# Cached keys and values of a decoder step moved through memory into longer rows, and the products on the keys begun two projections later

## The chip, the cores and the metric

The kernel runs on one core of a Trainium2 chip. The core has a matrix engine (TensorE, PE in the profile; its weight loads are PEld), a vector engine (DVE), a scalar engine (ACT), a general engine (GpSimd, POOL) and a queue engine (SyncE, SP) that here only issues DMAs. 16 DMA engines move data between the memory (DRAM tensors) and the on-chip buffer. The engines run side by side and wait for each other through semaphores. The metric is the device time of one execution in microseconds; three runs of the kernel before had a median of 1405.13 us (1403.96 to 1405.38).

## What is computed

One inference step of a one-layer decoder for a prompt of 1024 tokens and 8 sequences that each add 8 tokens to a long past. Of the layer, the attention matters here. It has three groups of four heads (width 64) with window and dilation (128, 1), (512, 4) and (2048, 16). A query at position t reads t, t−d, t−2d, ... back to t−window. For the 8 added tokens of each sequence the older keys and values come from caches:

```python
idx = Lw + jnp.arange(T)[:, None] - jnp.arange(band + 1)[None, :] * dil
kg = k_full[:, idxc].astype(F32)
vg = v_full[:, idxc].astype(F32)
s = jnp.einsum('bthd,btjhd->bthj', q.astype(F32), kg) * (HEAD_DIM ** -0.5)
p, lse = masked_softmax_stats(s, valid[None, :, None, :])
return jnp.einsum('bthj,btjhd->bthd', p, vg), lse
```

In the third group the dilation 16 is larger than the 8 new tokens, so each of the 64 sample queries (8 tokens x 8 sequences) has 128 cached keys of its own, which no other query shares. In the second group (dilation 4) queries share cached rows. The cache of a group lies in memory as position x sequence x 512 floats: 256 of the key (four heads) and then 256 of the value. So the key of one position is a run of 1 KB, and the value too. The rest of the layer (a pooling branch, gates, output projection, a feed-forward part) follows the attention.

## The kernel before

The whole layer is one program. First come the normaliser of the tokens and the projection of the pooling branch (up to about 60 us). Then a loop over the head groups in the order third, second, first (`for g in (2, 1, 0)`, L1141; group numbers in the code count from 0, so `g == 2` is the third group) computes q, k and v. In each group there are nine blocks: eight of 128 prompt tokens, b = 0 to 7, and block 8 with the 64 sample tokens. A call of `qkv_part` (L605) does one projection of one block: on PE 24 matmuls, of which those with q and k together ("wide", for blocks 1 to 5) have twice the columns. Blocks 8 and 0 are done as q, k, v in turn, blocks 1 to 5 as q with k and then v, blocks 6 and 7 as q of both, k of both, v of both. So each group has 3 + 10 + 6 = 19 projections of prompt blocks.

After a projection of q or k, ACT squares its result (L643 or L647), POOL adds a small term (L650, tile ms) and raises to the power −1/2 (L651, tile mr), and ACT scales the result by it (L656, tile qk). Transposes on PE follow (L672, tiles tqg2b, tqg1b), then scores (L689, sg2b), the running maximum on DVE (L698), the exponential on ACT (L699), transposes of the weights (L708, tpg2b), their copy from PSUM on ACT (L711) and the product with the values (L722, pog2b). L116 and L117 split a weight panel into a high and a low part on ACT and DVE. In the third group DVE also makes sums of tokens in a tile ts (L524 to L532) that SP stores to memory (L533, ts_d) before the tile is used again.

The order of the instructions on PE is that of the program. On the other engines a planner orders them by a simulated time line. `behind_pe` (L186) adds a wait for a given matmul, and so paces an instruction. `step` and `soon` run pieces of the other blocks' work between projections.

The sample queries of the third group are done by `sample_own_keys` (L849), a generator that is advanced by `own_step` (L1104), once after a projection (or in its middle, where it is wide) while the second and the first group are projected. It begins with a scaling of the queries on DVE (L862), which needs a loaded row wq. Then, for 16 pieces of four keys each: load the piece (`piece`, L840, tile pck, two DMAs of 256 KB on SP at L846, in runs of 1 KB), multiply it with the queries in four POOL instructions (L856), and add up on DVE (L869). After a softmax come 16 pieces of values (tile pcv), again four products each on POOL and sums on DVE (L894, L895). That makes 34 steps. The projections that have none are listed at L1200 and L1201.

The sample queries of the second and the first group are done by `sample_shared_keys` (L902). Its inner function `ask` (L910) loads keys (L927, from an input that is already transposed) and values (L923, tiles kt and keys, [128, 2 x 256] floats, in runs of 1 KB).

POOL issues DMAs of its own only late (L2115, from 454.9 us on: the shifted copies of the caches), on another queue than SP's.

Of the kernel before, what the change touches and what calls it, by code (L numbers as in the profile page):

```python
# [7 lines left out]
F32 = mybir.dt.float32  # L8
# [7 lines left out]
P = 128  # L16
D = 1024
SEQ = 1024
NB, NT = 8, 8
# [7 lines left out]
DIL = (1, 4, 16)  # L27
HD = 64
KPC = 4
# [8 lines left out]
def decoder_step(ctx, tc, i, o):  # L38
    nc = tc.nc
    v_, s_, g_, t_ = nc.vector, nc.scalar, nc.gpsimd, nc.tensor  # L40
    dma = nc.sync.dma_start
# [112 lines left out]
    def feed():  # L154
        while coming_up and coming_up[0]["key"] in ends_of:
            p = coming_up.pop(0)
            cs = slice(p["a"], p["a"] + 512)
            ins = split(p["wt"][:, 0, cs], p["wt"][:, 1, cs], p["raw"])
            behind_pe(ins, ends_of[p["key"]])
            if p["a"] + 512 == p["width"]:  # L160
                throttle.append(ins)
            ask_ahead()
# [21 lines left out]
    last_mm, last_norm = [None], [None]  # L184

    def behind_pe(ins, mm=None):  # L186

        tc.add_manual_dep(ins.ins, (mm or last_mm[0]).ins.name,
                          mybir.DependencyInfo(mybir.DependencyClass.Sync, mybir.DependencyReason.DATA), reason="pace")
# [17 lines left out]
    dp = pool("dram", space=DRAM)  # L207
# [14 lines left out]
    pg_d = dp.tile([8, P, H], F32, name="pg_d")  # L222
    ts_d = dp.tile([4, P, 4, H], F32, name="ts_d")
    new_d = dp.tile([NT, NB, 768], F32, name="new_d")
    so_d = [dp.tile([NT, NB, 4, 66], F32, name=f"so_d{g}") for g in range(2)]

    accs = ExitStack()
# [311 lines left out]
    ap = pb.enter_context(tc.tile_pool(name="att", bufs=1, reuse_waits="tile"))  # L539
# [300 lines left out]
    def piece(kv, j, name):  # L840
        t = rr(sp1, [P, KPC, 256], F32, name=f"pc{name}", tag="pc", bufs=2)
        src = i["cache_kv3"]
        for hf in range(2):
            a = bass.AP(tensor=src.tensor, offset=src.offset + (64 * hf + j) * DIL[2] * NB * 512 + kv * 256,
                        ap=[[512, NT * NB], [DIL[2] * NB * 512, KPC], [1, 256]])
            dma(t[64 * hf:64 * hf + 64], a)  # L846
        return t

    def sample_own_keys(qs, wq):  # L849
        g = 2  # L850
# [51 lines left out]
    def sample_shared_keys(g, qk, vt):  # L902
# [7 lines left out]
        def ask(n):  # L910
            if n >= len(order) or n in there:
                return
            bg, kv, r = order[n]
            there[n] = ts = []
            for x in range(2):
                if extra and x:
                    turn["extra"] = turn.get("extra", -1) + 1
                    t = extra[turn["extra"] % 3]
                else:
                    t = rr(sp, [P, 4 * 136], F32, name=f"kt{g}_{n}_{x}", tag="kt", bufs=3)  # L920
                if kv:
                    ts.append(t[:, :512].rearrange("p (b j) -> p b j", b=2))
                    dma(ts[x], i[f"cache_kv{g + 1}"].rearrange("(m r) b c -> r m b c", r=R)  # L923
                        [r][:, 4 * bg + 2 * x:4 * bg + 2 * x + 2, 256:])
                else:
                    ts.append(t.rearrange("p (b j) -> p b j", b=4))
                    dma(ts[x][:, :, :128], i[f"kT{g + 1}"][r, :, x, 4 * bg:4 * bg + 4, :])  # L927
# [213 lines left out]
    for g in (2, 1, 0):  # L1141
# [42 lines left out]
        for blks in ((8, 0), (1,), (2,), (3,), (4,), (5,)) + (((6, 7),) if g else ((6,), (7,))):  # L1184

            if g and 6 in blks:
                next_wts = [(place[0] + j) % 3 for j in range(3)]
                for j, after in enumerate((((7, 0, 1), (7, 0, 3), (6, 1, 1), (6, 1, 3)), ((7, 1, 1), (7, 1, 3), (6, 2, 1), (6, 2, 3)),
                                           ((7, 2, 0), (7, 2, 1), (7, 2, 2)))):
                    keys_of = [(g,) + a for a in after] + [(g - 1, 8, 1)] * (j == 2)  # L1190
                    line_up(i["w_in"][2 + 3 * j + g - 1], f"qkv{g - 1}_{j}", *keys_of)
            elif not g and 3 in blks:
                wg_first = line_up(lambda a: gate_quarter(a // 512 % 2, a // 1024), "ga0",
                                   *((0, 7, j) for j in (0, 0, 1, 1)), width=2048)
            tiles = {b: qkv_tiles(f"{g}_{b}", b == 8) for b in blks}

            for js in (((0, 1), (2,)) if blks[0] in (1, 2, 3, 4, 5) else ((0,), (1,), (2,))):
                for b in (blks[::-1] if g < 2 and js == (2,) and 8 in blks else blks):

                    own = g < 2 and (g, b, js) in ((0, 8, (0,)), (0, 8, (1,))) or g < 2 and b < 8 and (g, b, js) not in (  # L1200
                        (1, 7, (1,)), (1, 6, (2,)), (1, 7, (2,)), (0, 6, (0,)), (0, 6, (2,)), (0, 7, (2,)))  # L1201

                    def middle():
                        step()
                        if own:
                            own_step(1)

                    def quarter(q):
                        ends_of[g, b, js[0], q] = last_mm[0]
                        feed()  # L1210

                    if g == 1 and extra and (1, "keys") in done:
                        extra = []
                        natt = np_.tile([P, 8, 2, P], F32R, name="natt", tag="nat")
                        soon(lambda: in_order(0, (0, 2)), lambda: in_order(0, (4, 6)))
                    wide = len(js) == 2
                    qkv_part(g, wts, b, f"{g}_{b}", tiles[b], js, middle if wide else None,
                             quarter if g and b in (6, 7) else None)
                    feed()
                    if own and not wide:  # L1220
                        own_step(1)
                    if g < 2 and b == 8 and 0 in js:
                        dma(wrow, src_w)
                    if g == 0 and b == 8 and 2 in js:

                        sel = ap0.tile([P, 1024], F32R, name="sel", tag="smp")[:, :12 * HD]
                        pick = lambda a: lambda: behind_pe(v_.tensor_tensor(
                            sel[:, 256 * a:256 * a + 256].rearrange("p (a d) -> p a d", d=HD),
                            ident[:, 4 * a:4 * a + 4].unsqueeze(2).to_broadcast([P, 4, HD]),
                            ident[:, 12 + 4 * a:16 + 4 * a].unsqueeze(2).to_broadcast([P, 4, HD]), op=ALU.add))  # L1230
                        soon(pick(0), pick(1), pick(2))
                    if 2 in js:
                        (sample_block if b == 8 else prompt_block)(g, b, *tiles[b])
                if g == 2 and 8 in blks and js != (0,):
                    start(*((pool_branch(), "p") if 2 in js else (token_sums(), "t")), now=True)
# [981 lines left out]
```

## Time and profile before

| | |
|---|---|
| median of three runs | 1405.13 us |
| the profiled execution's own time | 1403.42 us |
| its span, first to last instruction | 1401.6 us |
| granted TensorE clock | 1.000 |
| third group's projections | about 60 to 160 us |
| second group's | about 160 to 270 us |
| first group's | about 270 to 380 us |
| moved by DMA in all | 303.57 MB, mean 217 GB/s |

The profile is of one execution. "Busy" is the time in which an engine executes an instruction; where a row ends in square brackets, the engine stood idle for that many microseconds before it, until the engine or the DMA named had finished. The chain that ended last is followed back from the last instruction, at each step to what released it. A window gives busy times in a stretch, and the share of time in which the 16 DMA engines had a packet in hand.

### The profile page before, as it was taken

What the parts mean: (1) busy time and instruction counts of PE and PEld (TensorE: products, weight loads), DVE (VectorE), ACT (ScalarE), POOL (GpSimd) and SP (SyncE); (2) the same over time, 40 slices, a digit from 0 to 9 for tenths busy, and PEclk for the clock granted to TensorE, in tenths of its full rate; (3) what the DMA queues carried; (4) which work ended last, traced back from release to release, by engine and by line L of the source; (5) the groups of instructions that cost most, each with busy time, mean ns of one, the idle gap of its engine ahead of it and who ended that gap; (6) DMA issues with size and microseconds to landing.
All of it is one profiled execution on the core that took longest, in us unless ns stands there. A gap on an engine that the chain in (4) does not pass through costs nothing.

```text
span 1401.6 us, 29306 instructions
## 1 busy us (share of the span) xinstructions
PE 1392.2 (99%) x11101; PEld 1342.7 (96%) x11101; DVE 954.3 (68%) x1714; ACT 754.5 (54%) x1778; POOL 236.2 (17%) x330
## 2 busy tenths in 40 slices
PE   9999999999999999999999999999999999999998
PEld 8988977887999999999999999999999999999998
DVE  7788744776776767875568677665665686664565
ACT  8557766687765323563336455555554544444443
POOL 0722266475500000000010000000000000000100
PEclk9999999999999999999999999999999999999999
DMA  6322788745477767965368668856758987777684
GB/s 215 117 90 102 220 228 215 216 127 144 120 254 232 253 216 250 319 227 179 130 203 285 227 221 269 269 200 210 249 189 287 325 272 261 234 243 231 206 260 168
DMA packets 184540, 303.57 MB, mean 217 GB/s; under 512 B 26567, under 2 KB 90509, under 8 KB 182350
## 3 DMA queue, kind: packets, MB, share of 16 engines
q1 hardware_dynamic: 181326, 258.04, 58.4%
q0 software_dynamic: 3072, 43.65, 9.8%
q8 instruction: 87, 1.43, 0.4%
q14 instruction: 55, 0.45, 0.1%
HBM read 231.55 MB, written 113.73 MB: 246 GB/s over the span
## 4 chain that ended last, share of the span: by engine, by line
PE 93%; DMA 2%; POOL 2%; DVE 1%; ACT 1%; issue 0%; SPq 0%; DVEq 0%; POOLq 0%
PE pz L1297 24%; PE pd L2075 24%; PE pg L1297 12%; PE ph L200 7%; PE pqk L200 5%; PE pab L1297 5%; PE pv L200 4%; PE a L328 3%; PE pq L200 1%; PE pk L200 1%; POOL pcv L856 1%; PE sg0b L689 1%; PE pog0b L722 1%; PE tpg0b L708 1%; POOL mr L651 0%; DMA ts_d<-ts 0%
## 5 line engine op out<-in xcount | busy, mean ns | idle before, releaser
L2075 PE MATMUL pd<-places 128*128 128x272 f32 x2688 | 331.7, 287 | 0.0
L2075 PEld LDWEIGHTS pd<-places 128*128 128x128 f32 x2688 | 331.6, 188 | 0.0
L116 ACT ACTIVATE places<-raw_d 128x544 fp32r<-128x544 f32 (+1 forms) x176 | 110.7, 646 | 162.7 <-DMA raw_d<-z_d 51.4
L117 DVE TENSOR_TENSOR places<-raw_d,places 128x544 fp32r<-128x544 f32 (+1 forms) x176 | 122.6, 712 | 92.4 <-ACT places L116 90.6
L2115 POOL DMA_DIRECT2D out_kv_sample_dram<-in_cache_kv_dram x96 | 47.2, 492 | 790.7 <-ACT places L116 580.9
L1297 PE MATMUL pz<-act,places 128*128 128x280 f32 (+1 forms) x1080 | 139.4, 287 | 0.0
L1297 PEld LDWEIGHTS pz<-act,places 128*128 128x128 f32 x1080 | 135.9, 188 | 0.0
L200 PE MATMUL ph<-act,places 128*128 128x280 f32 (+1 forms) x768 | 96.6, 287 | 0.0
L200 PEld LDWEIGHTS ph<-act,places 128*128 128x128 f32 x768 | 96.0, 188 | 0.1
L1297 PE MATMUL pg<-act,places 128*128 128x264 f32 (+1 forms) x576 | 75.6, 288 | 0.0
L1297 PEld LDWEIGHTS pg<-act,places 128*128 128x128 f32 x576 | 72.6, 188 | 0.6 <-issue 0.3
L1297 PE MATMUL pz<-places,apart 128*128 128x264 f32 (+1 forms) x528 | 67.9, 287 | 0.0
L1297 PEld LDWEIGHTS pz<-places,apart 128*128 128x128 f32 x528 | 66.6, 188 | 0.0
L200 PE MATMUL pqk<-places,act 128*128 128x512 f32 x240 | 60.6, 402 | 0.6 <-ACT qk L656 0.6
L1297 PE MATMUL pz<-act,apart 128*128 128x264 f32 (+1 forms) x456 | 59.2, 287 | 0.0
L1297 PEld LDWEIGHTS pz<-act,apart 128*128 128x128 f32 x456 | 57.5, 188 | 0.3 <-ACT e L1862 0.2
L200 PEld LDWEIGHTS pqk<-places,act 128*128 128x128 f32 x240 | 44.7, 192 | 10.5 <-ACT qk L656 0.8
L651 POOL TENSOR_TENSOR mr<-ms,mhalf 128x4 f32<-128x4 f32 (+2 forms) x39 | 52.9, 1356 | 3.1
L856 POOL TENSOR_TENSOR pck<-pck,qs 128x256 f32<-128x256 f32 x64 | 47.4, 774 | 29.1 <-DMA pck<-in_cache_kv_dram 24.5
L328 PE MATMUL a<-act,places 128*128 128x384 f32 (+1 forms) x288 | 50.3, 332 | 0.9 <-ACT act L306 0.4
L1297 PE MATMUL pab<-ab,places 128*128 128x264 f32 (+1 forms) x384 | 50.4, 286 | 0.0
L328 PEld LDWEIGHTS a<-act,places 128*128 128x128 f32 x288 | 47.5, 188 | 2.8 <-ACT act L306 1.2
(435 smaller groups left out, 2789.3 us busy)
## 6 DMA issues: line engine op xcount, KB each, us to landing
out_kv_sample_dram<-in_cache_kv_dram POOLq DMA_DIRECT2D x72, 480.0 KB, 4.9
raw_d<-z_d SPq DMA_DIRECT2D x112, 272.0 KB
z_d<-t SPq DMA_DIRECT2D x80, 272.0 KB
raw_d<-in_w_down_dram SPq DMA_DIRECT2D x80, 256.0 KB
raw_u<-in_w_up_dram SPq DMA_DIRECT2D x64, 256.0 KB
raw_qkv<-in_w_in_dram SPq DMA_DIRECT2D x36, 256.0 KB
pck<-in_cache_kv_dram SPq DMA_DIRECT2D x32, 256.0 KB
pcv<-in_cache_kv_dram SPq DMA_DIRECT2D x32, 256.0 KB
```

Of the source, the lines that this page charges most:

```text
L116: ins = s_.activation(dst_hi, src, AF.Copy)
L117: v_.tensor_tensor(dst_lo, src, dst_hi.bitcast(F32), op=ALU.subtract)
L200: last_mm[0] = t_.matmul(out, lhs(a, k), rhs(b, k), start=(j == 0), stop=(j == len(terms) - 1))
L328: last_mm[0] = t_.matmul(pts[m][:, :n], wt[:, a, kk, m * P:(m + 1) * P], act4[b][kk][:, :, part4(c)], start=(p == 0 and kk == 0), stop=(p ...
L651: last_norm[0] = g_.tensor_tensor(r[:n, :H], ms[:n, :H], mhalf[:n, :H], op=ALU.pow)
L689: t_.matmul(sc[e][:, hp, j * P:(j + 1) * P], qT[rows, hp, :], kT[rows, 2 + hp, :], start=True, stop=True)
L708: t_.transpose(tp[:, hp * nk + j, :], sms[e][:, hp, j * P:(j + 1) * P], ident)
L722: t_.matmul(po[e * HD:(e + 1) * HD, hp, :], vr[:, h * HD:(h + 1) * HD], pTs[e][:, hp * nk + j, :], start=(j == 0), stop=(j == nk - 1))
L856: ins = g_.tensor_tensor(out, *others, op=ALU.mult)
L1297: last_mm[0] = t_.matmul(out[c], lhs(*term), rhs(*term, c), start=(first and n == 0), stop=(n == len(terms) - 1), skip_group_check=not first)
L2075: last_mm[0] = t_.matmul(outs(chain[t], Q)[c], A[:, a, t * P:(t + 1) * P], Z[:, b, c], start=(fresh and f == 0 and n == 0), stop=(f == NG ...
L2115: ins = g_.dma_start(d, a)
```

## The change

Two sets of buffers in memory are added, 16 of 512 KB for the third group's keys (`own_d`) and 16 of 256 KB for the second group's values (`val_d`). While the third group is projected, POOL issues DMAs from memory to memory that copy the caches into them, three after each of its first 16 projections of prompt blocks: two for one piece of four keys, one for one piece of values. Each waits for the last matmul that stood ahead of the projection (`before[0]`). The pieces of keys are then loaded in one DMA with rows of 4 KB, the second group's values in rows of 2 KB. The values of the third group and those of the first are loaded as before.

The list of projections without a step of the own keys changes: block 0's q and k in the second group have none now, and block 7's k in the second group and block 6's q in the first have one. The number of steps stays 34.

```diff
+    own_d = [dp.tile([P, KPC * 256], F32, name=f"own_d{n}") for n in range(16)]
+    val_d = [dp.tile([P, 512], F32, name=f"val_d{n}") for n in range(16)]
...
     def piece(kv, j, name):
         t = rr(sp1, [P, KPC, 256], F32, name=f"pc{name}", tag="pc", bufs=2)
         src = i["cache_kv3"]
+        if not kv:
+            dma(t.rearrange("p n d -> p (n d)"), own_d[j // KPC])
+            return t
         for hf in range(2):
             a = bass.AP(tensor=src.tensor, offset=src.offset + (64 * hf + j) * DIL[2] * NB * 512 + kv * 256,
                         ap=[[512, NT * NB], [DIL[2] * NB * 512, KPC], [1, 256]])
             dma(t[64 * hf:64 * hf + 64], a)
         return t
+
+    before = [None]
+
+    def shared_values(g, bg, r, x):
+        return i[f"cache_kv{g + 1}"].rearrange("(m r) b c -> r m b c", r=DIL[g])[r][:, 4 * bg + 2 * x:4 * bg + 2 * x + 2, 256:]
+
+    def own_rows():
+        src = i["cache_kv3"]
+        row = DIL[2] * NB * 512
+        for n in range(16):
+            for hf in range(2):
+                a = bass.AP(tensor=src.tensor, offset=src.offset + (64 * hf + n * KPC) * row,
+                            ap=[[512, NT * NB], [row, KPC], [1, 256]])
+                behind_pe(g_.dma_start(own_d[n][64 * hf:64 * hf + 64].rearrange("p (n d) -> p n d", n=KPC), a), before[0])
+            r, bx = n % 4, n // 4
+            behind_pe(g_.dma_start(val_d[4 * r + bx].rearrange("p (b d) -> p b d", b=2), shared_values(1, bx // 2, r, bx % 2)),
+                      before[0])
+            yield
+
+    own_moves = own_rows()
...
-                    dma(ts[x], i[f"cache_kv{g + 1}"].rearrange("(m r) b c -> r m b c", r=R)
-                        [r][:, 4 * bg + 2 * x:4 * bg + 2 * x + 2, 256:])
+                    if g:
+                        dma(t[:, :512], val_d[4 * r + 2 * bg + x])
+                    else:
+                        dma(ts[x], shared_values(g, bg, r, x))
...
-                        (1, 7, (1,)), (1, 6, (2,)), (1, 7, (2,)), (0, 6, (0,)), (0, 6, (2,)), (0, 7, (2,)))
+                        (1, 0, (0,)), (1, 0, (1,)), (1, 6, (2,)), (1, 7, (2,)), (0, 6, (2,)), (0, 7, (2,)))
...
+                    before[0] = last_mm[0]
                     qkv_part(g, wts, b, f"{g}_{b}", tiles[b], js, middle if wide else None,
                              quarter if g and b in (6, 7) else None)
                     feed()
+                    if g == 2 and b < 8:
+                        next(own_moves, None)
```

## The prediction

> **What bounds the kernel now.** I read the page first (busy time, then the chain that ended last), then the windows by stage, then the waits of the weight loads and the timeline at the places where TensorE stops.
>
> ```profile
> span 1401.6 us, 29306 instructions
> PE 1392.2 (99%) x11101; PEld 1342.7 (96%) x11101; DVE 954.3 (68%) x1714; ACT 754.5 (54%) x1778; POOL 236.2 (17%) x330
> PE 93%; DMA 2%; POOL 2%; DVE 1%; ACT 1%; issue 0%; SPq 0%; DVEq 0%; POOLq 0%
> ...
> 63.00:78.00 15.00, 15.00 (x116) 14.23 (x117) 7.82 (x27) 8.51 (x52) 8.58 (x10) 1.00 0.18 54
> 78.00:90.00 12.00, 12.00 (x67) 10.10 (x65) 11.53 (x19) 5.97 (x35) 2.44 (x2) 1.00 0.24 81
> 90.00:101.50 11.50, 11.50 (x73) 9.90 (x72) 10.35 (x27) 7.82 (x42) 2.61 (x2) 1.00 0.21 75
> 101.50:113.00 11.50, 11.50 (x74) 9.61 (x74) 11.08 (x25) 8.05 (x44) 2.81 (x2) 1.00 0.32 120
> 113.00:125.00 12.00, 12.00 (x80) 10.19 (x79) 10.08 (x23) 7.89 (x41) 2.14 (x2) 1.00 0.38 138
> 125.00:137.00 12.00, 12.00 (x85) 10.07 (x84) 10.19 (x23) 8.48 (x43) 3.31 (x2) 1.00 0.20 70
> 170.00:260.00 90.00, 89.00 (x757) 71.21 (x756) 45.97 (x135) 56.44 (x228) 57.24 (x79) 1.00 0.88 224
> 262.00:272.00 10.00, 8.07 (x78) 6.99 (x71) 8.03 (x20) 7.25 (x22) 5.14 (x7) 1.00 0.83 229
> 410.00:420.00 10.00, 10.00 (x83) 10.00 (x82) 8.93 (x15) 7.46 (x16) 0.00 (x0) 1.00 0.97 318
> ```
>
> The columns of the windows are: stretch, its length, busy time of PE, PEld, DVE, ACT and POOL, the granted clock, the share of the DMA engines, GB/s. TensorE is busy 1392.2 of 1401.6 us, at clock 1.00, and has 93% of the chain. So nothing but idle TensorE can be won. The third group's projections (63 to 160 us) keep PE full, with DVE next (11.08 of 11.50 us) and the DMA engines at 0.18 to 0.38. In the second group (170 to 260 us) the DMA engines are at 0.88, yet PE is idle for 1.00 us of 90. The other loss is at 262 to 272 us: 1.93 us. Those idle times have causes in the timeline:
>
> ```profile
> 172.04 0.43 DVE L862 SCALAR_TENSOR_TENSOR qs<-wq,qs 128x256 f32<-128x256 f32 x1 [2.20 <-DMA wq<-in_qk_norm_dram]
> 173.94 2.80 POOL L856 TENSOR_TENSOR pck<-pck,qs 128x256 f32<-128x256 f32 x4 [3.34 <-DVE ss L873]
> 174.22 0.40 ACT L699 ACTIVATE smg2b<-smg2b,sta 128x128 f32<-128x128 f32 x1 [2.66 <-DVE sta L698]
> 174.77 0.14 PEld L708 LDWEIGHTS tpg2b<-cst,smg2b 128*128 128x128 f32 x1 [0.55 <-ACT smg2b L699]
> 175.15 0.14 PEld L708 LDWEIGHTS tpg2b<-cst,smg2b 128*128 128x128 f32 x1 [0.25 <-ACT smg2b L699]
> 178.04 0.91 ACT L656 ACTIVATE qk<-pk,mr 64x64 f32<-64x64 f32 x4 [1.63 <-POOL mr L651]
> 179.00 2.60 PEld L200 LDWEIGHTS pqk<-places,act 128*128 128x128 f32 x12 [0.83 <-ACT qk L656]
> ...
> 265.38 0.63 ACT L116 ACTIVATE places<-raw_qkv 128x512 fp32r<-128x512 f32 x1 [2.23 <-PE pv L200]
> 268.54 0.41 ACT L711 COPY pTg1b<-tpg1b 128x256 f32<-128x256 f32 x1
> 269.00 0.41 PEld L722 LDWEIGHTS pog1b<-pTg1b,v 128*64 128x64 f32 x6 [2.17 <-ACT pTg1b L711]
> ```
>
> The reader is to see two stalls. At 174 to 179 us the weight loads wait 0.55 + 0.25 + 0.83 = **1.63 us**. DVE had stood 2.20 us at L862, the first work of the third group's own keys, for a DMA; L698, L699 and the transposes came late behind it, and POOL's first four key products (2.80 us) stood ahead of the normaliser that L656 waits for. At 269 us they wait **2.17 us** for one PSUM copy, which stands in ACT's order behind a weight split (L116) that had waited for PE's own projection. Together 3.80 us, 0.27% of the time: that is about the most a change here can gain.
>
> **The change part by part.**
>
> *Key products begun two projections later.* The own-key steps of the second group's first block, parts q and k, go; two come back at its block 7, k, and the first group's block 6, q. The count stays 34, so the work is moved and not removed: each step is 4 products on POOL, a reduction on DVE and a load. What leaves the 174 to 179 us stretch is L862's wait (2.20 us), L862 and the first products. DVE, then L698 and L699, come about 2.20 + 0.43 = 2.6 us earlier, more than the 1.63 us that PE waits, and POOL's 2.80 us no longer stand ahead of mr. I take the whole 1.63 us; next late there is PE itself. Bounds: 0 (the planner puts something else there) to −1.63. The last step with keys and the softmax fall one step each into the first group, where POOL has room:
>
> ```profile
> 272.00:282.00 10.00, 10.00 (x94) 9.66 (x93) 7.75 (x14) 7.39 (x22) 1.30 (x3) 1.00 0.65 172
> ```
>
> POOL is busy 1.30 of 10 us, so 2.80 us more are covered; if they weren't, the normalisers after 282 us would be late by up to 2.8 us.
>
> *The 48 moves, on POOL.* 16 calls, one behind each of the third group's first 16 projections, issue two moves of keys and one of values, 256 KB each in 1 KB pieces from memory to memory: 12.6 MB. Each waits for a matmul that precedes its projection, so it is ready when POOL is idle, and the ms and mr (L650, L651) that follow on POOL queue behind it; ACT's L656 waits for these. No row shows a POOL move of this shape. The nearest:
>
> ```profile
> L2115 POOL DMA_DIRECT2D out_kv_sample_dram<-in_cache_kv_dram x96: 488/488/717, 454.9 to 1335.0; - x96
> L846 SPq DMA_DIRECT2D pck<-in_cache_kv_dram x32: 596/608/1007, 167.0 to 256.5; - x32
> q0 software_dynamic: 3072, 43.65, 9.8%
> L650 POOL TENSOR_TENSOR ms<-ms,stats 128x8 f32<-128x8 f32 x5 | 3.5, 696 | 45.9 <-ACT qk L647 45.9
> 71.67 0.19 POOL L650 TENSOR_TENSOR ms<-ms,stats 64x4 f32<-64x4 f32 x1 [2.41 <-ACT qk L647]
> 85.14 0.45 POOL L650 TENSOR_TENSOR ms<-ms,stats 128x8 f32<-128x8 f32 x1 [9.89 <-ACT qk L647]
> 85.67 1.99 POOL L651 TENSOR_TENSOR mr<-ms,mhalf 128x8 f32<-128x8 f32 x1
> 87.70 1.75 ACT L656 ACTIVATE qk<-pqk,mr 128x64 f32<-128x64 f32 x8 [0.40 <-POOL mr L651]
> 94.15 0.60 PE L672 MATMUL tqg2b<-cst,qk 128*128 128x128 f32 x4
> ```
>
> Lower end: 488 ns, POOL's own move (few, long pieces). Upper end: if all of that is per packet, 3072/96 = 32 packets make 15 ns each, and 256 pieces with 16 packets more 4.1 us. I take **0.61 us**, the row with the same source, bytes and pieces (L846, though on SP's queue). 48 x 0.61 = 29 us. POOL's idle time per block is 45.9/5 = 9.2 us, for 6 moves 3.7 us: covered. A normaliser that falls behind three moves is late by at most 1.8 us; its transposes have 94.15 − (87.70 + 1.75) = 4.7 us to spare. Cost 0. Cover is gone at 9.2/6 = 1.5 us a move, and at the opening, where 12 moves share 2.41 + 9.89 = 12.3 us, at 1.0 us.
>
> *The 48 moves, on the DMA engines.* q0's 43.65 MB took 9.8% of 1401.6 us: 318 GB/s. 12.6 MB are 40 us, over some 80 us in which the engines stand at about 0.3; the sum is 0.8. A call's three moves are a burst of 2.5 us. They hide behind PE; the stores that DVE waits for are the danger (below).
>
> *Larger rows in the second group.* 16 loads of 512 KB in place of 32 of 256, and 16 value loads in 2 KB rows: the same bytes, SP saves 16 x 0.61 us. PE's 1.00 us there hangs on the first stall already counted. So 0.
>
> The Trainium skill, "DMA: Bandwidth & Descriptors", Specifications, puts line rate at rows of 512 B and more, which speaks against this part: 1 KB would be enough already. Here 224/0.88 = 255 GB/s per full share at 170 to 260 us stand against 318/0.97 = 328 at 410 us, so the trace rather disagrees; by either the sum keeps a 0 here.
>
> Sum: −1.63 us. For the second stall I take 0, as none of the ACT work in front of L711 is taken away; ends −2.17 and, for another like it made by the new order, +2.17. The profiled execution took 1403.42 us (span 1401.6 and 1.8 around it), 1.7 below the median 1405.13; 1403.42 − 1.63 = 1401.8, against the median **1403.5 us**.
>
> **The rivals.**
>
> *Both stalls go.* Fewer issues on SP and quicker loads shift the order at 262 us, too: −3.80, so 1401.3 (−0.27%). For it: POOL's steps and their loads move exactly there. Against: the split that holds ACT waited for PE.
>
> *POOL becomes the bound* (slower). The place is ms and mr behind the moves; it decides at 1.0 us a move for the opening, 1.5 us for the blocks. At 1.7 us the opening lacks 12 x 1.7 − 12.3 = 8.1 us, less 4.7 spare, and each of 4 further blocks 6 x 1.7 − 9.2 = 1.0: +7.4 − 1.6 = +5.8, so 1410.9. At 4.1 us the opening lacks 36.9 us and each of the 4 blocks 15.4: about +95. For it: POOL operations already stretch here, the same 128x8 sum takes from 0.30 to 1.31 us:
>
> ```profile
> 119.90 0.30 POOL L650 TENSOR_TENSOR ms<-ms,stats 128x8 f32<-128x8 f32 x1 [9.16 <-ACT qk L647]
> 131.50 1.31 POOL L650 TENSOR_TENSOR ms<-ms,stats 128x8 f32<-128x8 f32 x1 [9.38 <-ACT qk L647]
> ```
>
> Against: L2115's minimum and median are both 488 ns.
>
> The Trainium skill, "SBUF — State Buffer", the box on DVE blocking DMA, says that a move issued from POOL can't write its descriptors while DVE runs a two-port copy, some 0.62 us becoming 3.1 us; 48 x 3.1 = 149 us would be this rival at its worst. Its section Who interferes with whom exempts a tensor_tensor, which is most of what DVE does here; no run shows it either way.
>
> *The stores wait* (slower). DVE reuses the ts tile (L524) once its store landed, and has little to spare:
>
> ```profile
> DVE ts L524 <- DMA ts_d<-ts: 3.9, 4, 1.5
> 149.06 5.91 DMA ts_d<-ts
> ```
>
> Eight stores, each behind a burst of 2.5 us, are 20 us at most; DVE is idle 59 − 53.2 = 5.8 us at 78 to 137 us. With half of them caught, 10 − 5.8 = +4.2, less 1.6: 1407.7. Against: PE has slack of its own.
>
> *The change doesn't do what it says*: the planner leaves the first products where PE waits as before. 1405.1.
>
> **How the numbers follow.** A measurement of this kernel tells 0.2% (2.8 us) from no change. Forecast 0.40, no effect 0.06, both stalls gone 0.22, POOL bound 0.19, stores 0.13. So faster 0.22, same 0.46, slower 0.32. The range: below it goes past both stalls by 0.4 us, 1400.9; above to 1412.0, which takes in the stores and POOL up to 1.7 us a move, and leaves out moves beyond that. Cases of both signs share it; the likeliest one's own range is 1402.3 to 1405.7 (−2.8 to +0.5).
>
> **What would show it.** Right: POOL's move rows at 0.5 to 1.0 us; no wait of weight loads on L699 or L656 near 175 us; L862 without a wait for wq; mr rows of the third group at most 2 us later than now; DMA share 0.6 to 0.9 at 78 to 137 us. Wrong: move rows over 1.0 us with L656 waiting for mr and PE for L656 or L672; L524 waiting for ts_d over 1.5 us; a new wait of 2 us on PE from the planner's order.

## The result, and the profile after

The changed kernel is slower. Its median is 1410.61 us (1408.06 to 1414.16, 11 runs), that of the kernel before, run beside it, 1406.71 us (1403.58 to 1409.57, 11 runs). The ratio is 1.0027, 95% interval 1.0015 to 1.0039. The forecast was 1403.5 us against 1405.13, 0.9988.

The page of the changed kernel, its first lines (span, busy time of each engine):

```profile
span 1408.4 us, 29343 instructions
PE 1394.1 (99%) x11101; PEld 1343.0 (95%) x11101; DVE 959.2 (68%) x1714; ACT 755.3 (54%) x1778; POOL 267.3 (19%) x378
```

POOL is busy 31.1 us longer (267.3 against 236.2), and has 48 instructions more: the moves. The number of matmuls is the same. The stretches that the prediction showed are these in the changed kernel (length, busy time of PE, PEld, DVE, ACT, POOL, granted clock, share of the DMA engines, GB/s):

```profile
63.00:78.00 15.00, 13.42 (x104) 12.38 (x102) 6.61 (x23) 8.57 (x57) 12.57 (x17) 1.00 0.47 148
78.00:90.00 12.00, 12.00 (x75) 10.86 (x74) 9.38 (x17) 4.50 (x26) 5.91 (x11) 1.00 0.88 280
90.00:101.50 11.50, 9.56 (x55) 7.35 (x54) 9.23 (x20) 5.52 (x35) 5.24 (x6) 1.00 0.61 196
...
137.00:160.00 23.00, 22.18 (x185) 20.61 (x185) 18.22 (x46) 18.02 (x86) 15.30 (x19) 1.00 0.90 276
170.00:260.00 90.00, 89.25 (x767) 72.01 (x766) 46.71 (x142) 57.37 (x231) 50.93 (x68) 1.00 0.72 219
262.00:272.00 10.00, 10.00 (x100) 8.32 (x98) 8.30 (x14) 6.92 (x20) 8.90 (x11) 1.00 0.89 305
```

The reader is to see where PE's column falls short of the length. Before the change PE was full from 63 to 160 us; the last of these stretches in the kernel before:

```profile
137.00:160.00 23.00, 23.00 (x191) 21.24 (x191) 17.89 (x47) 19.81 (x88) 6.42 (x8) 1.00 0.59 180
```

Now PE lacks 1.58 us at 63 to 78, 1.94 at 90 to 101.5 and 0.82 at 137 to 160. The second group at 170 to 260 us, busy in its DMA engines for 0.88 before, is at 0.72 now. The stall near 269 us is gone; in its place PE waits 1.0 us for a copy of the same kind (L713) near 282 us.

Because all kernels of this study issue the same 11101 matmuls in the same order, each matmul can be compared with itself: its start after the first matmul, less the same in the kernel before. That difference at a few places, taken as growth over a stretch of the kernel before, says where time is lost (+) or won (−):

```
us of shift against before     60 to 170   170 to 190   190 to 280   280 to the end
changed kernel                    +5.24       -0.63        -1.42        +2.98
```

So the third group loses 5.24 us, the second group wins 2.05, and a further 2.98 are lost later, spread over a stretch where the change does no more than let the own-key steps come one projection later, up to the first group's block 6. The profiled execution of before (1403.42 us) is some 3 us faster than the medians of its later runs (1405.94 to 1406.9); the sum of such a row, +6.78 with the first 60 us, reads too high by about that. The last column is the least certain: one execution of each kernel, and no experiment below takes it apart.

The three places of the third group, in the timeline of the changed kernel (start, length, engine, line; in brackets the idle time before and what ended it):

```profile
63.56 1.36 POOL L866 DMA_DIRECT2D own_d<-in_cache_kv_dram  x2 [1.20 <-PE mt L401]
65.42 3.48 POOL L404 TENSOR_TENSOR stats<-xg,mhalf 128x8 f32<-128x8 f32 x2
68.67 0.53 POOL L652 TENSOR_TENSOR ms<-ms,stats 64x4 f32<-64x4 f32 x2
69.61 1.24 POOL L866 DMA_DIRECT2D own_d<-in_cache_kv_dram  x2 [0.41 <-PE pk L624]
70.78 0.76 POOL L868 DMA_DIRECT2D val_d<-in_cache_kv_dram  x1
71.35 2.22 POOL L653 TENSOR_TENSOR mr<-ms,mhalf 64x4 f32<-64x4 f32 x2
74.10 1.72 ACT L658 ACTIVATE qk<-pq,mr 64x64 f32<-64x64 f32 x8
75.07 0.39 PE L624 MATMUL pv<-places,smp_t 128*128 128x256 f32 x1 [1.58 <-ACT qk L658]
...
89.02 1.36 DVE L526 TENSOR_TENSOR ts<-act,act 128x544 f32<-128x544 f32 x2 [2.39 <-DMA ts_d<-ts]
91.30 2.21 POOL L653 TENSOR_TENSOR mr<-ms,mhalf 128x8 f32<-128x8 f32 x1
96.55 0.27 DVE L700 CUSTOM_DVE_ANT_0 smg2b<-sg2b,cst 128x128 f32<-128x128 f32 x1
96.87 0.40 ACT L701 ACTIVATE smg2b<-smg2b,sta 128x128 f32<-128x128 f32 x1 [1.99 <-DVE sta L700]
97.27 1.73 ACT L658 ACTIVATE qk<-pqk,mr 128x64 f32<-128x64 f32 x8
98.64 0.95 PE L674 MATMUL tqg2b<-cst,qk 128*128 128x128 f32 x4 [1.86 <-ACT qk L658]
...
152.07 0.91 PE L509 MATMUL pl<-ext,lin 128*128 128x384 f32 x2 [0.82 <-DVE ext L484]
```

The same place in the kernel before:

```profile
67.00 1.00 POOL L651 TENSOR_TENSOR mr<-ms,mhalf 64x4 f32<-64x4 f32 x1
68.04 0.91 ACT L656 ACTIVATE qk<-pq,mr 64x64 f32<-64x64 f32 x4 [0.39 <-POOL mr L651]
72.48 0.52 PE L622 MATMUL pv<-places,smp_t 128*128 128x256 f32 x1
```

Six moves stand ahead of the first mr. The three of the first call, from 63.56 us on, stand ahead of POOL's work on the tokens' statistics (L404). The three of the second call, from 69.61 us on, stand between two ms and the two mr that belong to them. The mr begin at 71.35 us; before, the first was at 67.00 us (0.61 us of the difference is there on PE, too, at 60 us). ACT's scaling L658 is late behind them, at 74.10 in place of 68.04 us. PE's next projection of v needs the PSUM that L658 reads. Before, it came 3.5 us after the end of that scaling (72.48 less 68.95); now it waits 1.58 us. At 91.3 us the same order delays an mr; the planner then put L658 on ACT behind one exponential L701. This waits for L700 on DVE, and DVE had stood 2.39 us for the store of ts. PE waits 1.86 us. At 152 us PE waits 0.82 us for DVE alone. (The line numbers are higher behind the added code: L650, L651, L656, L672, L711 and L722 are now L652, L653, L658, L674, L713 and L724.)

The moves themselves, and DVE's waits for the stores between 60 and 180 us (us in total, times, longest):

```profile
L866 POOL DMA_DIRECT2D own_d<-in_cache_kv_dram x32: 585/619/742, 63.6 to 147.8; - x32
L868 POOL DMA_DIRECT2D val_d<-in_cache_kv_dram x16: 723/758/795, 64.8 to 148.4; - x16
DVE ts L526 <- DMA ts_d<-ts: 10.6, 6, 2.6
```

A move costs POOL 0.62 or 0.76 us. The stores are waited for 10.6 us in place of 3.9.

### The profile page after: what moved, and what is told of

It is laid out like the page before. It is cut to its first block, busy times and chain, and to the rows that moved or that the text cites. A ratio compares the mean times of both kernels' runs of the same rounds, so it can differ in the third digit from the quotient of the medians.

```text
span 1408.4 us, 29343 instructions
## 1 busy us (share of the span) xinstructions
PE 1394.1 (99%) x11101; PEld 1343.0 (95%) x11101; DVE 959.2 (68%) x1714; ACT 755.3 (54%) x1778; POOL 267.3 (19%) x378
## 4 chain that ended last, share of the span: by engine, by line
PE 70%; DMA 2%; DVE 1%; ACT 0%; issue 0%; SPq 0%; DVEq 0%; ACTq 0%
PE pz L1327 23%; PE pd L2105 21%; PE pg L1327 12%; PE ph L200 7%; PE pab L1327 4%; DMA raw_d<-in_w_down_dram 1%; DMA raw_d<-z_d 1%; PE pog0b L724 0%; DVE places L117 0%; PE sg0b L691 0%; PE tpg0b L710 0%; ACT places L116 0%; PE pk L200 0%; PE pv L200 0%; PE pq L200 0%
## 5 line engine op out<-in xcount | busy, mean ns | idle before, releaser
L653 POOL TENSOR_TENSOR mr<-ms,mhalf 128x4 f32<-128x4 f32 (+2 forms) x39 | 53.3, 1374 | 2.5 <-POOL ms L652 0.2
```

Of the source, the lines that this page charges most:

```text
L653: last_norm[0] = g_.tensor_tensor(r[:n, :H], ms[:n, :H], mhalf[:n, :H], op=ALU.pow)
```

## The experiments

Two theories stood against each other. **Order**: the moves delay the normalisers on POOL, and the order that the planner makes around them leaves PE waiting, whatever the moves carry. **Bytes**: 12.6 MB of copies hold up the stores and loads of the third group. Beside them stood the question of what the own steps and the longer rows bring. The shifts of all runs, as above, with the recorded ratio to the runs of before that were made beside each. (It is not the ratio of the two medians, which differs from it by up to 0.001.)

```
                     60 to 170  170 to 190  190 to 280  280 to end   ratio to before, 95% interval
changed kernel         +5.24      -0.63       -1.42       +2.98      1.0027  [1.0015, 1.0039]
e1_steps_only           0.00      -1.88       +1.21       +1.40      0.9980  [0.9971, 0.9989]
e2_moves_only          +7.78      +3.60       -2.01       +1.48      1.0049  [1.0036, 1.0062]
e3_behind_norm         +7.36      -0.50       -1.77       +1.82      1.0037  [1.0025, 1.0050]
e4_dead_moves          +7.02      -0.56       +2.90       +1.13      1.0053  [1.0039, 1.0067]
e8_short_moves         +3.69      -0.44       +1.56       -0.81      1.0011  [0.9997, 1.0024]
e9_norm_short          +5.02      -1.89       +0.47       +5.51      0.9995  [0.9982, 1.0008]
e10_values_only        +0.23      -1.88       +1.93       +2.34      0.9989  [0.9975, 1.0004]
e11_keys_only          +0.08      -1.89       -1.37       +0.74      0.9976  [0.9958, 0.9993]
e12_third_short        +2.83      -0.22       -0.66       -0.60      0.9999  [0.9987, 1.0010]
e5_moves_on_sp         +2.56      -1.50       -1.56       +0.48      0.9990  [0.9975, 1.0004]
e13_keys_old_steps     +0.32      +0.26       -2.32       +0.05      0.9991  [0.9972, 1.0010]
```

One thing in these shifts is neither order nor bytes as such. In the profiled executions of six kernels the granted clock of PE fell to 0.5 for 3.41 us right behind a stall. In e1_steps_only:

```profile
264.05:267.47 3.42, 1.44 (x12) 1.07 (x10) 2.56 (x6) 3.22 (x10) 2.49 (x4) 1.00 1.10 231
267.47:270.88 3.41, 3.03 (x15) 2.70 (x16) 3.41 (x12) 3.41 (x13) 1.51 (x3) 0.50 0.40 112
```

Over such a stretch the shift grows by 1.3 to 1.6 us more. In the first column this is in e2, e3, e4 and e9, in the second in e2, in the third in e1, e4 and e10. The kernel before, the changed kernel, e5, e8, e11, e12 and e13 have no such stretch between 60 us and the last 20 us, so they can be compared as they stand.

**The two halves of the change.** e1_steps_only is the kernel before with the new list of own steps and no move. e2_moves_only is the changed kernel with the old list.

```diff
-                        (1, 7, (1,)), (1, 6, (2,)), (1, 7, (2,)), (0, 6, (0,)), (0, 6, (2,)), (0, 7, (2,)))
+                        (1, 0, (0,)), (1, 0, (1,)), (1, 6, (2,)), (1, 7, (2,)), (0, 6, (2,)), (0, 7, (2,)))
```

> The kernel before with only the list of own-key steps changed: no move, loads as before. Order theory (the moves on POOL stand ahead of the normalisers ms and mr, which come late): the third group loses nothing, so PE comes to the second group's first projections (174.8 us before) within 0.5 us of before; the stall of 1.63 us at 174 to 179 us shrinks by 0.5 to 1.6 us and the whole is 0 to 4 us faster than before. Traffic theory (the moves' bytes delay the stores that DVE waits for): the same, as there are no moves. Chance theory (any new order of the planner costs some us): the third group may lose 2 to 5 us here as well.

> The moves and the longer rows with the own-key steps where they were before. Order and traffic theory: the third group loses what it lost in the changed kernel, 5.2 us (PE 5 to 6 us late at the second group's start), and the whole is 4 to 7 us slower than before. If the loss came from the later key steps: the third group loses nothing.

The steps alone made the kernel faster, 0.9980; the moves alone slower, 1.0049. In e1 nothing changes up to 170 us, and between 170 and 190 us 1.88 us are won: the weight loads' waits for L699 and L656 are gone. Part of it comes back behind that: +1.21 us between 190 and 280, at the second stall. There PE's weight load waits 2.6 us in place of 2.2, and 1.3 us more are lost at the halved clock behind it. So the loss belongs to the moves. (Of e2's shift up to 190 us, 2.8 us are the clock's.)

**The moves behind the normaliser.** In e3_behind_norm each move also waits for the mr of its block, so that POOL takes it up behind that.

```diff
+    def after_norm(ins):
+        behind_pe(ins, before[0])
+        behind_pe(ins, last_norm[0])
...
-                behind_pe(g_.dma_start(own_d[n][64 * hf:64 * hf + 64].rearrange("p (n d) -> p n d", n=KPC), a), before[0])
+                after_norm(g_.dma_start(own_d[n][64 * hf:64 * hf + 64].rearrange("p (n d) -> p n d", n=KPC), a))
```

> The changed kernel, but each set of three moves also waits for the normaliser mr of the projection that it follows, so that POOL takes it behind mr. Order theory: the waits of PE for the scaled q and k near 75 and 98 us (2.0 and 2.3 us) go; the third group ends at most 1.5 us later than before, and the whole is 3 to 5 us faster than the changed kernel. Traffic theory: as many bytes in the same time, DVE still waits 8 to 11 us for the stores of ts, and the third group is still 3 to 5 us late.

The two stalls at 75 and 99 us are gone; the shift does not grow at all up to 101 us. But the third group ends 7.36 us late, up to 1.6 us of it by the halved clock. The waits of PE and DVE in e3_behind_norm, 60 to 180 us:

```profile
PE pl L509 <- DVE ext L484: 2.6, 1, 2.6
PE sg2b L691 <- DVE qkTg2b L677: 1.7, 2, 1.1
...
DVE ts L526 <- DMA ts_d<-ts: 13.6, 7, 3.9
```

PE now waits for DVE, and DVE for the stores. Order explains the first two stalls, and with them gone something else of the moves still costs time. That the moves run later here, up to 160 us in place of 148, next to more of the stores, was not separated from it.

**The moves without their readers.** e4_dead_moves makes all 48 moves, but keys and values are loaded from the caches in runs of 1 KB as before the change.

```diff
-        if not kv:
-            dma(t.rearrange("p n d -> p (n d)"), own_d[j // KPC])
-            return t
...
-                    if g:
-                        dma(t[:, :512], val_d[4 * r + 2 * bg + x])
-                    else:
-                        dma(ts[x], shared_values(g, bg, r, x))
+                    dma(ts[x], shared_values(g, bg, r, x))
```

> The changed kernel, all moves made, but keys and values loaded from the caches in 1 KB rows as before, so the copies are not read. If the longer rows bring anything, this is slower than the changed kernel by that: 1 us or more. My theory: the same as the changed kernel within 1 us in the profile's stages (third group 5.2 us late), since PE waits for none of these loads.

1.0053 against 1.0027: reading the copies is worth some 3.7 us to the changed kernel. In the shifts they are seen between 190 and 280 us, +2.90 in place of −1.42 (1.5 us of e4's +2.90 are the clock's). The prediction's sum had 0 for them, and so had the theory on record for e4.

**Short moves.** e8_short_moves is e4 with only the first 32 floats of each run moved; e9_norm_short does the same behind the normaliser.

```diff
-                            ap=[[512, NT * NB], [row, KPC], [1, 256]])
+                            ap=[[512, NT * NB], [row, KPC], [1, 32]])
```

> The 48 moves stay where the changed kernel has them, but each copies only the first 32 floats of a piece (128 bytes in place of 1 KB) and nothing reads the copies: the second group's value tiles and the third group's key tiles are loaded from the caches in 1 KB pieces as before the change. Theory A, POOL's and ACT's order makes the loss of the third group: the two stalls near 75 and 99 us stay at 2.0 and 2.8 us, the third group ends some 5 us late, VectorE still waits for ts_d about as long as in e4_dead_moves (10.5 us) only if the count of pieces counts. Theory B, the bytes make the loss: the wait for ts_d falls to about 4 us as before the change, the stall behind VectorE's ext near 152 us (1.0 to 1.2 us) goes, and the third group ends 2 us earlier than with whole moves. Time by A 1.005 of before, by B 1.002.

> As e8_short_moves, but each set of moves also waits for the normaliser of its block, as in e3_behind_norm. If order and bytes together make the whole loss of the third group, then there is nothing left of it: TensorE's matmuls up to 200 us are within 1 us of before the change, VectorE's wait for ts_d is near 4 us, ScalarE's wait for sta near its value before, and the time is that of e1_steps_only, 0.997 to 0.999 of before. If the count of moves or of pieces costs by itself, the end of the third group stays 5 us or more late, as in e3 (7.6 us), and the time is 1.003 to 1.005.

With an eighth of the bytes the stall at 75 us stays (a step of 1.98 us in the shift), while what is lost from 79 to 101 us shrinks from 4.66 us in e4 (3.2 without the halved clock) to 1.52. The third group loses 3.69 us in place of 7.02 (5.55 without it). DVE's wait for ts_d is 4.5 us in place of 10.5. So both theories hold a part: neither the order nor the bytes is the whole. In e9 nothing is lost up to 140 us (0.01 us of shift), as expected, but then a single stall of 2.87 us comes, which neither theory had, and 1.6 us of halved clock behind it. ACT and PE in e9_norm_short, near it:

```profile
165.32 0.35 ACT L713 COPY pTg2b<-tpg2b 128x256 f32<-128x256 f32 x1
167.97 0.63 ACT L116 ACTIVATE places<-raw_qkv 128x512 fp32r<-128x512 f32 x1 [2.29 <-DMA raw_qkv<-in_w_in_dram]
168.51 0.35 ACT L713 COPY pTg2b<-tpg2b 128x256 f32<-128x256 f32 x1
168.91 1.11 PE L724 MATMUL pog2b<-pTg2b,v 128*64 128x128 f32 x6 [2.75 <-ACT pTg2b L713]
```

The copy that PE waits for (168.51 us) stands behind a weight split that waits 2.29 us for its load: the form of the old second stall, made anew by the planner's order. e9 says the losses up to 140 us are explained; it does not reproduce e1.

**Keys alone, values alone.** e10_values_only keeps the 16 moves of values and loads the keys as before. e11_keys_only keeps the 32 moves of keys and loads the values as before. So each has one or two moves in a step in place of three.

```diff
-            r, bx = n % 4, n // 4
-            behind_pe(g_.dma_start(val_d[4 * r + bx].rearrange("p (b d) -> p b d", b=2), shared_values(1, bx // 2, r, bx % 2)),
-                      before[0])
...
-                    if g:
-                        dma(t[:, :512], val_d[4 * r + 2 * bg + x])
-                    else:
-                        dma(ts[x], shared_values(g, bg, r, x))
+                    dma(ts[x], shared_values(g, bg, r, x))
```

(e11; e10 leaves out the loop over hf and the three lines in `piece` instead.)

> The changed kernel with the 16 moves of values alone; the third group's keys are loaded from the cache as before. A third of POOL's moves and of their bytes is left (11.6 us of POOL, 4.2 MB). If the loss goes with the moves' number, the third group ends 1 to 2 us late in place of 5; if one move ahead of a normaliser is enough for the stall, the stalls at 75 and 99 us stay at a third to the whole of 2.0 and 2.3 us. The gain of the second group near 270 us (2 us) stays if it is the value rows that bring it, and goes if it is the key rows. With both in its favour 0.997 of before, with both against it 1.003.

> The changed kernel with the 32 moves of keys alone; the second group's values are loaded from the cache as before. Two thirds of the moves stay (18.9 us of POOL, 8.4 MB). By the number of moves the third group ends 3 to 4 us late. The gain near 270 us stays if the key rows bring it and goes if the value rows do. 1.001 to 1.004 of before.

Neither loses anything in the third group: +0.23 and +0.08. With two thirds of the moves and of their bytes a loss of 3 to 4 us was expected, so the loss does not go with their number. The keys' moves bring the gain near 270 us (−1.37), the values' do not (+1.93, or +0.5 without the halved clock; e1, without any move, has −0.1 so). **e11_keys_only has the lowest ratio of the study, 0.9976**; its interval ends at 0.9993, and that of the changed kernel begins at 1.0015. Whether it beats e1_steps_only (0.9980) these runs can't tell: by the medians alone e1, e10, e11 and e13 all lie between 0.9981 and 0.9984. Its timeline at the place of the first stall:

```profile
69.35 0.62 POOL L866 DMA_DIRECT2D own_d<-in_cache_kv_dram  x1 [1.06 <-PE pk L624]
69.99 1.04 POOL L653 TENSOR_TENSOR mr<-ms,mhalf 64x4 f32<-64x4 f32 x1
70.99 0.62 POOL L866 DMA_DIRECT2D own_d<-in_cache_kv_dram  x1
71.63 1.05 POOL L653 TENSOR_TENSOR mr<-ms,mhalf 128x4 f32<-128x4 f32 x1
...
71.06 0.91 ACT L658 ACTIVATE qk<-pq,mr 64x64 f32<-64x64 f32 x4
73.83 0.97 ACT L658 ACTIVATE qk<-pq,mr 128x64 f32<-128x64 f32 x4
```

With two moves the planner puts one ahead of each mr, not all ahead of both. The first L658 begins at 71.06 us in place of 74.10, and PE does not wait.

**A third move without bytes.** e12_third_short is e11 with a third move at the place of the value move, 128 bytes a run, that nobody reads. POOL and ACT have the changed kernel's order in the third group again.

```diff
+            behind_pe(g_.dma_start(val_d[n].rearrange("p (b d) -> p b d", b=2)[:, :, :32],
+                                   shared_values(1, n // 4 // 2, n % 4, n // 4 % 2)[:, :, :32]), before[0])
             yield
```

> e11_keys_only with a third move in each step, at the place of the value move, that copies 128 bytes of each piece (0.5 MB in all) and that nobody reads. In the third group POOL's and ScalarE's instructions stand in the order of the changed kernel again, while the bytes are nearly those of e11_keys_only. Theory A, the third instruction on POOL and the order that the planner makes of it cost the changed kernel its time: the stalls near 75 us (2.0 us) and 98 us (1 to 2.3 us) are back, the third group ends 3 to 4 us late, and the time is 1.000 to 1.002 of before. Theory B, it is the bytes of the value moves: no stall at 75 and 98 us, and 0.997 to 0.998 of before as in e11_keys_only.

Theory A's stalls are back. The waits of PE and DVE in e12_third_short, 60 to 180 us:

```profile
PE pv L624 <- ACT qk L658: 1.6, 1, 1.6
PE tqg2b L674 <- ACT qk L658: 0.3, 1, 0.3
...
DVE ts L526 <- DMA ts_d<-ts: 6.7, 6, 1.7
```

The stall at 75 us is exactly that of the changed kernel (1.6 us on PE). The one at 99 us is 0.3 in place of 1.9 us: with the same order it needs DVE's long wait for a store, too. By 190 us e12 stands 4.4 us behind e11 (+2.61 against −1.81): the price of the third instruction and its order. Of these, 2.75 us are lost in the third group and 1.67 between 170 and 190 us, where no move is issued any more (the last at 146.7 us). The changed kernel stands another 2.0 us behind (+4.61): the price of the values' bytes. POOL's order is the same in both; DVE's is not, and its part in the 2.0 us is not separated. e8 does not fit quite as well: with fewer bytes than e12 it ends the third group 0.9 us later; that is left open.

**The moves on SP.** e5_moves_on_sp issues the 48 moves from SP.

```diff
-                behind_pe(g_.dma_start(own_d[n]...
+                behind_pe(dma(own_d[n]...
```

> The changed kernel with all 48 moves issued from SP's queue in place of POOL, so that no normaliser has a move ahead of it; bytes, sizes and readers as changed. Theory A: the stalls at 75 and 98 us go, and what is left is the traffic's part; from e9_norm_short and e3_behind_norm that is 1 to 3 us of waits for ts_d and ext. Time 0.998 to 1.001 of before. Theory B: the third group ends 5 us late or later, as in the changed kernel. A wait of a move on SP for its matmul holds the loads queued behind it, which can cost a stall for weights in either theory.

With every byte and no move on POOL the stalls at 75 and 99 us are gone, and what the third group loses, 2.56 us, is waited for on DVE (ts_d 8.5 us; PE waits 0.9 us for L677). The ratio is 0.9990 in place of 1.0027. This is a second measure of the bytes, beside the 2.0 us above.

**The keys' rows alone.** e13_keys_old_steps is e11 with the old list of steps.

> e11_keys_only with the list of own steps as before the change: the keys' moves and their 4 KB rows alone. If the two halves of the gain add up (the steps bring the stall of 174 to 184 us, the rows that of 269 us), the stall at 174 to 184 us is back (1.3 us or more over e11), the one at 269 us is smaller by 1 to 2 us than before the change, and the time is 0.998 to 1.000 of before. If the longer rows bring nothing, the time is 1.000 to 1.001; e4_dead_moves against the changed kernel, 1.0053 to 1.0027, speaks for 2 to 4 us by the rows of keys and values together.

As expected the first stall is back (+0.26 in place of −1.89), and the second stall is nearly gone: −2.32 us. The time, 0.9991, is not told from no change. ACT at the second stall in e13_keys_old_steps:

```profile
263.74 0.63 ACT L116 ACTIVATE places<-raw_qkv 128x512 fp32r<-128x512 f32 x1 [2.29 <-DMA raw_qkv<-in_w_in_dram]
...
265.33 1.78 ACT L603 CAST natt<-act 128x256 fp32r<-128x256 f32 x3
266.99 0.41 ACT L713 COPY pTg1b<-tpg1b 128x256 f32<-128x256 f32 x1
```

Before, a second weight split stood ahead of this copy, begun at 265.38 us, and the copy began at 268.54. Here only one stands there, and the copy begins 1.55 us earlier. So this gain came through another order on ACT; the split's own wait for its load is no shorter (2.29 us against 1.54). With the same order, e1 and e11 show the loads at work. In e1_steps_only, SP's issue of the weight panel and the split that waits for it:

```profile
257.14 0.58 SPq L127 DMA_DIRECT2D raw_qkv<-in_w_in_dram  x1
264.25 0.63 ACT L116 ACTIVATE places<-raw_qkv 128x512 fp32r<-128x512 f32 x1 [2.95 <-DMA raw_qkv<-in_w_in_dram]
```

In e11_keys_only:

```profile
256.77 0.57 SPq L127 DMA_DIRECT2D raw_qkv<-in_w_in_dram  x1
262.17 0.63 ACT L116 ACTIVATE places<-raw_qkv 128x512 fp32r<-128x512 f32 x1 [2.02 <-DMA raw_qkv<-in_w_in_dram]
```

From issue to split it is 7.1 us in e1 and 5.4 in e11, and the wait of PE's weight load for the copy behind it falls from 2.6 to 1.0 us. In e10, with the keys in runs of 1 KB too, the split waited 4.0 us for its load.

## Why the prediction was wrong

**The stall at 174 to 179 us** was forecast to go whole, −1.63 us. In e1, e10 and e11 it does: −1.88 to −1.89. In the changed kernel only 0.63 us are won, and 0.22 in e12, because the wait of PE's weight load for L658 stays (0.8 and 1.0 us). No move stands ahead of that normaliser, as the last is issued at 148.4 us. In e5 and e9 1.50 and 1.89 are won, but in e3, where the moves stand behind the normalisers as in e9, only 0.50. So the step was right by itself, and how the moves took most of it back in some kernels is not shown.

**"The 48 moves, on POOL: covered. Cost 0"** is the step that failed. The price of a move was right (0.61 forecast, 0.62 and 0.76 measured), and so was the room: POOL was not full. What failed is how the delay of mr was priced. The prediction took three moves ahead of one mr, 1.8 us, and set them against the 4.7 us that one block's transposes had to spare. The trace shows a start later by 4.35 us for the first mr (71.35 against 67.00), because six moves stand ahead of it: the planner put the first call's three ahead of L404 and the second call's three ahead of two normalisers at once, and these waited for PE besides. It shows another reader with less to spare: PE's projection of v, which needs the PSUM that L658 empties, had 3.5 us. And it shows that ACT's order moves with POOL's, so that near 99 us L658 came behind work that waits for DVE. The bound "cover is gone at 1.0 us a move" was a bound on POOL's capacity; the loss began at 0.62 us with three moves, and was nothing with two. The rival "POOL becomes the bound" named the place (L656 late behind ms and mr, PE late for L656 or L672) but not the point from which it decides. Price by e12 against e11: 4.4 us, 2.75 of it in the third group.

**"They hide behind PE; the stores that DVE waits for are the danger"**: the danger was real, together with the order. The rival gave +4.2 us; the bytes cost 2.0 us (the changed kernel against e12) or 2.56 (e5). Two thirds of the bytes in the same stretch cost 0.08 us (e11). There the stores are waited for 6.6 us, and PE does not see it.

**"Larger rows in the second group: 0"** was a term set to nothing that is worth some 2 to 4 us: −2.32 in e13 alone, 3.7 us by e4 against the changed kernel. It comes from the keys' loads, not from the values'. The prediction's sum argued that PE's 1.00 us hung on the first stall and counted the second as unchanged, with ends of 2.17 us either way; only its rival "Both stalls go" had quicker loads at the second stall, with 0.22. What of the loads did it stays open: a piece of keys was two loads of 64 partitions in runs of 1 KB out of the cache, and became one of 128 partitions in rows of 4 KB out of a compact copy. No run separates these. The queue of SP's loads from 172 to 276 us, before and in e11_keys_only (packets, MB, share of the 16 engines' time):

```profile
q1 hardware_dynamic: 29149, 22.88, 85.5%
```

```profile
q1 hardware_dynamic: 23159, 23.23, 72.7%
```

For 23 MB the engines are busy 0.727 of the stretch in place of 0.855. Per busy time that is 23.23/(0.727 x 104 us) = 307 GB/s against 22.88/(0.855 x 104) = 257. That is a rise by 19% for the whole queue; e11 has the new steps, too, and against e1, which has them without the moves, it is 307 against 265. The Trainium skill, "DMA: Bandwidth & Descriptors", Specifications, puts line rate at 512 B and more. By it rows longer than 1 KB would bring nothing; the trace shows a rise, but not that the length of the rows made it, as the loads changed in more than that.

**"Next late there is PE itself"** holds for 170 to 190 us only. The own-key work that left this stretch makes the second stall longer by 0.4 us where the keys are loaded as before (e1), and the halved clock behind it costs 1.3 us more in that execution. With the new steps and the keys' new loads together (e11) the wait is 1.0 us, and the clock stays at 1.00.

**The worst case of POOL** did not appear. The Trainium skill, "SBUF — State Buffer", A bandwidth-pool intuition that's wrong, gives about 3.1 us for a POOL-issued DMA that a copy on DVE holds up. The longest issue of the 48 moves took 0.795 us in the changed kernel and 1.025 in e3_behind_norm, with DVE busy for 9.38 of 12 us at 78 to 90 us in the changed kernel.

**The chances**: 0.32 stood on the slower side, split between the two rivals that, together, took place; they were held apart as if only one could. Both follow from one thing, a third move in each step. That the measured 1410.61 us stands so near the 1410.9 of "POOL becomes the bound" is luck: that sum took 1.7 us a move, and a move took 0.62 or 0.76.

What is left open: the 2.98 us of shift behind 280 us in the one profiled execution of the changed kernel, the 0.9 us between e8 and e12, the first stall in e3 against e9, and what of the keys' new loads makes them quicker.

## What to carry to other kernels

An engine with idle time is not free to issue DMAs: ask what its next instruction releases, on which engine that stands in what order, and who waits for the PSUM that it empties; the smallest of these margins is the price, not the engine's idle share. Where a planner orders the other engines, one instruction more can change the order of several of them, so try such an addition in doses (here two moves a step cost nothing and three cost over 4 us) before it is judged. Longer and fewer loads were worth making here for the keys, whose loads crowd a busy stretch (32 of 256 KB became 16 of 512 KB), and brought nothing for the values. And before shifts between two profiles are compared, look at the granted clock behind each stall.

## What the runs showed of the hardware

The issue of a move on POOL does not go by its bytes. The value moves took 723/758/795 ns (least, median, most) with runs of 1 KB. In e12_third_short they carry 128 bytes a run:

```profile
L867 POOL DMA_DIRECT2D val_d<-in_cache_kv_dram x16: 719/759/798, 64.8 to 146.7; - x16
```

The same 759 ns, for an eighth of the bytes. The key moves, of as many runs and bytes in another shape (64 x 4 runs in place of 128 x 2), took 619 ns, and 616 with 128 bytes a run (e8_short_moves). Such moves also leave their bytes behind: 2.9/4.1/7.3 us from issue to landing for the keys. With 12.6 MB in some 85 us DVE waits up to 2.6 us at a time for the stores of another queue, in place of 1.5.

A stall of PE can cost more than its length. Between 60 us and the end the profiles have eight stretches of 3.41 us in which PE stood idle for 1.97 us or more, in e1, e2, e3, e4, e9 and e10. Behind each of them the clock was granted at 0.5 for the next 3.41 us, and the shift grew by 1.3 to 1.6 us. Behind stretches with at most 1.58 us of idle time it stayed at 1.00 there. That is no threshold: at the start of e8_short_moves 1.52 us were followed by 0.5 as well.
